# Binary cross entropy over 8192 x 8192: the pieces of the small chunk move from GpSimd's DMA queue to SyncE's

## The chip, the core and the metric

The kernel runs on one core of a Trainium2 chip. A core has a tensor engine (unused here), VectorE (DVE), ScalarE (ACT), GpSimd (POOL) and SyncE (SP), and 16 DMA engines that move data between the chip's memory and the core's on-chip memory (128 partitions). Transfers are issued by an engine into its queue: q0 is the queue that GpSimd feeds by software, q1 the one that SyncE feeds. The metric is the device time of one execution in microseconds (us); the median of three runs is compared.

## The reference

```python
def setup_inputs():
    return {
        "pred": np.random.uniform(0.01, 0.99, (8192, 8192)).astype(np.float32),
        "target": np.random.randint(0, 2, (8192, 8192)).astype(np.float32),
    }

def reference(pred, target):
    eps = 1e-7
    pred = np.clip(pred, eps, 1 - eps)
    return -(target * np.log(pred) + (1 - target) * np.log(1 - pred))
```

Each target is 0 or 1, so each output is -log of the distance |target - 1 + pred|: that is pred where the target is 1 and 1 - pred where it is 0. Two arrays of 268 MB are read and one of 268 MB is written.

## The kernel before

The 8192 x 8192 elements are 524,288 columns on 128 partitions. `plan` (L20 to L27) cuts them into 37 chunks: two halves of 7,680 columns, 32 of 15,360, two halves of 7,680 again and one small one of 2,048. Two rings in on-chip memory hold two big chunks and the small one each: `ring_p` (float32: pred, worked on in place, then the output) and `ring_t` (bfloat16: target, converted by the transfer).

For a chunk, or half of it, `front_of` (L99) does two passes on DVE (L100: clip; L103: t - 1 + p) and two on ACT (L106: absolute value; L107: logarithm), and `back_of` (L109) one on DVE (L110: times -1). `load(k)` issues target and pred of chunk k on GpSimd, but the pred of chunk 0 on SyncE. `store(k)` issues on GpSimd, and on SyncE for the last chunks, k >= n - 3; the two that this concerns are a = 34 and b = 35. The order is written out by hand from L119 on; each engine does its part in this order and waits on semaphores for data, for free places in the rings, and for a semaphore that is used again. There are eight semaphores for the transfers of each of the two queues, taken in turn: the ninth transfer of a queue's turn waits until the first has landed.

In the loop (L133) chunk k is computed in halves and stored whole; behind `store(k)` the load of chunk k + 2 is issued, whose pred part waits for `store(k)` to land, since it takes its place. The small chunk (n - 1) is computed in the loop's turn k = 4.

The small chunk is loaded and stored in another shape. `mixed` (L81) lets partition 8a + b hold row 16b + a of 2,048 columns. Its pred and its output move in uneven pieces ("teeth"): a piece (j, lo, hi) is 32 partitions, 32j to 32j + 31, by columns 256 lo to 256 hi. On the side of the chip's memory it is 4 x 8 rows, on the on-chip side 32. `EARLY` lists the seven pieces of the load (widths in units of 256 columns: 8, 6, 4, 2, then 6, 4, 2), `LATE` the eight of the store (8, 1, 4, 6, 6, 1, 2, 4); either list makes up the small chunk. Before the change the first four loads are issued on GpSimd behind the first three chunks' loads (L122), the last three at L132, behind the load of chunk 3; the eight stores at L152, behind the second half store of z = 33.

The end (L144 to L158): z is computed in halves and stored in halves, a whole, b with its front in halves and its back (L157) and store whole.

Of the kernel before, what the change touches and what calls it, by code (L numbers as in the profile page):

```python
# [1 line left out]

# [4 lines left out]

EPS = 1e-7

BIG = 15 * 1024  # L10
HALF = BIG // 2
STEP = 256
EARLY = ((0, 0, 8), (1, 0, 6), (2, 0, 4), (3, 0, 2), (3, 2, 8), (2, 4, 8), (1, 6, 8))
LATE = (
    (0, 0, 8), (1, 0, 1), (2, 0, 4), (3, 0, 6),
    (1, 2, 8), (1, 1, 2), (3, 6, 8), (2, 4, 8),
)


def plan(total):  # L20

    n, last = divmod(total, BIG)
    assert n > 4 and 0 < last <= 2048
    spots = [(HALF, 0), (HALF, HALF)]
    spots += [(BIG, k % 2 * BIG) for k in range(1, n - 1)]
    end = (n - 1) % 2 * BIG
    return spots + [(HALF, end), (HALF, end + HALF), (last, 2 * BIG)]  # L27

@with_exitstack
def kernel(
    ctx: ExitStack,
    tc: tile.TileContext,
    pred: bass.AP,
    target: bass.AP,
    out: bass.AP,
):
    nc = tc.nc
    fp32 = mybir.dt.float32  # L40
    bf16 = mybir.dt.bfloat16
    Alu = mybir.AluOpType
    Act = mybir.ActivationFunctionType
    P = nc.NUM_PARTITIONS

    R, C = pred.shape
    spots = plan(R * C // P)
    n = len(spots)
    widths = [w for w, _ in spots]
    cols = [sum(widths[:k]) for k in range(n)]  # L50

    def chunk(ap, k):
        flat = ap.rearrange("r c -> (r c)")
        end = R * C - cols[k] * P
        return flat[end - widths[k] * P : end].rearrange("(p w) -> p w", p=P)

    pool = ctx.enter_context(tc.tile_pool(name="rings", bufs=1))
    ring = [P, 2 * BIG + widths[-1]]
    ring_p = pool.tile(ring, fp32, name="ring_p", tag="ring_p")
    ring_t = pool.tile(ring, bf16, name="ring_t", tag="ring_t")  # L60
    warm = pool.tile([1, 8], fp32, name="warm", tag="warm")

    def spot(ring, k, part=(0, 1)):
        w, c = spots[k]
        i, m = part
        return ring[:, c + i * w // m : c + (i + 1) * w // m]

    def load(k):
        queue = nc.sync if k == 0 else nc.gpsimd
        nc.gpsimd.dma_start(out=spot(ring_t, k), in_=chunk(target, k))  # L70
        queue.dma_start(out=spot(ring_p, k), in_=chunk(pred, k))  # L71

    def store(k, part=(0, 1)):
        queue = nc.sync if k >= n - 3 else nc.gpsimd
        i, m = part
        w = widths[k] // m
        queue.dma_start(  # L77
            out=chunk(out, k)[:, i * w : (i + 1) * w], in_=spot(ring_p, k, part)
        )

    def mixed(ap):  # L81
        flat = ap.rearrange("r c -> (r c)")[: widths[-1] * P]
        return flat.rearrange("(b a w) -> a b w", b=8, a=16)

    def tooth_of(ap, j, lo, hi):
        return mixed(ap)[4 * j : 4 * j + 4, :, lo * STEP : hi * STEP]

    def tooth_in(j, lo, hi):
        return spot(ring_p, n - 1)[32 * j : 32 * j + 32, lo * STEP : hi * STEP]

    def load_teeth(teeth):
        for tooth in teeth:
            nc.gpsimd.dma_start(out=tooth_in(*tooth), in_=tooth_of(pred, *tooth))  # L93

    def store_teeth(teeth):
        for tooth in teeth:
            nc.gpsimd.dma_start(out=tooth_of(out, *tooth), in_=tooth_in(*tooth))  # L97

    def front_of(p, t):  # L99
        nc.vector.tensor_scalar(  # L100
            out=p, in0=p, scalar1=EPS, scalar2=1 - EPS, op0=Alu.max, op1=Alu.min
        )
        nc.vector.scalar_tensor_tensor(  # L103
            out=p, in0=t, scalar=1.0, in1=p, op0=Alu.subtract, op1=Alu.add
        )
        nc.scalar.activation(out=p, in_=p, func=Act.Abs)  # L106
        nc.scalar.activation(out=p, in_=p, func=Act.Ln)  # L107

    def back_of(p):  # L109
        nc.vector.tensor_scalar(out=p, in0=p, scalar1=-1.0, scalar2=None, op0=Alu.mult)  # L110

    def front(k, *part):
        front_of(spot(ring_p, k, *part), spot(ring_t, k, *part))

    def back(k, *part):
        back_of(spot(ring_p, k, *part))

    with tc.manual_schedule():
        nc.vector.memset(warm, 1.0)  # L119
        for k in range(3):  # L120
            load(k)
        load_teeth(EARLY[:4])  # L122
        nc.scalar.activation(out=warm, in_=warm, func=Act.Ln)  # L123
        front(0)
        front(1)
        back(0)
        store(0)
        back(1)
        store(1)
        load(3)  # L130
        nc.gpsimd.dma_start(out=spot(ring_t, n - 1), in_=mixed(target))  # L131
        load_teeth(EARLY[4:])  # L132
        for k in range(2, n - 4):  # L133
            front(k, (0, 2))
            front(k, (1, 2))
            back(k, (0, 2))
            back(k, (1, 2))
            store(k)
            for j in range(k + 2, n - 1 if k == n - 5 else k + 3):
                load(j)  # L140
            if k == 4:
                front(n - 1)
                back(n - 1)
        z, a, b = range(n - 4, n - 1)  # L144
        front(z, (0, 2))
        front(z, (1, 2))
        back(z, (0, 2))
        store(z, (0, 2))
        front(a)
        back(z, (1, 2))  # L150
        store(z, (1, 2))
        store_teeth(LATE)  # L152
        front(b, (0, 2))
        front(b, (1, 2))
        back(a)
        store(a)
        back(b)  # L157
        store(b)  # L158


# [1 line left out]
_INS = ['pred', 'target']  # L162
_OUTS = [((8192, 8192), 'float32')]


# [23 lines left out]
```

## Time and profile before

| | |
|---|---|
| median of 3 runs | 1867.51 us (1867.19 to 1867.58) |
| profiled execution | 1866.22 us, span 1864.3 us |
| read and written in the chip's memory | 536.87 MB and 268.44 MB, 432 GB/s over the span |
| one pass over 7,680 columns | L100 4.16, L103 8.16, L110 4.16 us (DVE); L106 6.60, L107 6.60 us (ACT) |
| one pass over 3,840 columns | L100 2.16, L103 4.16 us (DVE); L106 3.39, L107 3.40 us (ACT) |
| big pred load, issue to landing (median) | 35.9 us |
| big store on q0, issue to landing (median) | 29.2 us |
| store of a and of b on q1, issue to landing (median) | 12.8 us |
| pieces: loads, issue to landing | 38.6 to 76.0 us |
| pieces: stores, issue to landing | 10.5 to 16.4 us |

The span is the profiled execution from the first to the last recorded instruction; the time of the execution has 1.9 us more around it. A line of the page's groups has the source line, the engine, the operation, what it writes and reads, the number of instructions, their busy time and mean duration, and the idle time before them with what ended it. In the waits the columns are who waited, for whom, the total in us, how often, and the longest. In a timeline they are start, duration, engine, line, operation and in brackets the idle time before and what ended it; several instructions in a row are merged, so that the duration then reaches from the start of the first to the end of the last. In the table of windows "x" is the number of instructions, and the last two columns are the mean busy share of the 16 DMA engines and what they moved.

### The profile page before, as it was taken

The numbers are of one execution on the slowest core, as the hardware profiler recorded it, in microseconds if no ns is written. First come the engines' busy times: TensorE is split into PE (matmuls) and PEld (weight loads), VectorE is DVE, ScalarE is ACT, GpSimd is POOL, SyncE is SP. The second block draws the span as 40 slices with busy tenths as digits, with TensorE's granted clock in tenths as the row PEclk, the third lists the DMA queues.
The fourth block names the chain that finished last, engine by engine and source line by source line (L and its number), as shares of the span: only waits on it lengthen the run. The fifth ranks groups of instructions, "written<-read, shape, count | busy, mean of one in ns | idle before, by whom it ended". The sixth has DMA issues, their size and how long they took to land.

```text
span 1864.3 us, 640 instructions
## 1 busy us (share of the span) xinstructions
DVE 1122.4 (60%) x210; ACT 900.0 (48%) x142; POOL 68.6 (4%) x126
## 2 busy tenths in 40 slices
DVE  4646676555666555566665556666555766555585
ACT  3345553345554334555433455543345554334555
POOL 1000000000000000000000000000000000000001
DMA  9999999999999999999999999999999999999999
GB/s 295 370 340 353 344 358 380 387 358 351 353 344 358 381 388 362 347 352 345 357 381 388 363 345 355 344 357 383 384 364 345 352 345 357 384 384 365 345 344 390
DMA packets 17620, 671.14 MB, mean 360 GB/s; under 512 B 3152, under 2 KB 3152, under 8 KB 3600
## 3 DMA queue, kind: packets, MB, share of 16 engines
q0 software_dynamic: 17184, 659.31, 98.7%
q1 hardware_dynamic: 432, 11.80, 1.5%
q14 instruction: 4, 0.03, 0.0%
HBM read 536.87 MB, written 268.44 MB: 432 GB/s over the span
## 4 chain that ended last, share of the span: by engine, by line
DMA 35%; issue 25%; ACT 23%; DVE 15%; POOL 1%; POOLq 0%; DVEq 0%; PEldq 0%
DMA ring_p<-in_pred_dram 32%; ACT ring_p L106 12%; ACT ring_p L107 11%; DVE ring_p L103 7%; DVE ring_p L100 4%; DVE ring_p L110 4%; DMA out_dram<-ring_p 3%; POOL ring_t L70 1%; POOL out_dram L77 0%; POOL ring_p L71 0%; POOLq L77 0%; DVEq L100 0%; POOLq L71 0%; PEldq L184 0%; POOLq L70 0%
## 5 line engine op out<-in xcount | busy, mean ns | idle before, releaser
L106 ACT ACTIVATE ring_p<-ring_p 128x7680 f32<-128x7680 f32 (+2 forms) x70 | 450.6, 6437 | 943.1 <-DVE ring_p L103 943.1
L103 DVE SCALAR_TENSOR_TENSOR ring_p<-ring_t,ring_p 128x7680 f32<-128x7680 bf16 (+2 forms) x70 | 557.2, 7960 | 2.4
L100 DVE TENSOR_SCALAR ring_p<-ring_p 128x7680 f32<-128x7680 f32 (+2 forms) x70 | 284.0, 4058 | 395.9 <-DMA ring_p<-in_pred_dram 395.9
L110 DVE TENSOR_SCALAR ring_p<-ring_p 128x7680 f32<-128x7680 f32 (+1 forms) x69 | 284.1, 4117 | 328.9 <-ACT ring_p L107 328.9
L107 ACT ACTIVATE ring_p<-ring_p 128x7680 f32<-128x7680 f32 (+2 forms) x70 | 451.1, 6444 | 2.2
L71 POOL DMA_DIRECT2D ring_p<-in_pred_dram x35 | 18.7, 534 | 921.7 <-DMA out_dram<-ring_p 921.7
L77 POOL DMA_DIRECT2D out_dram<-ring_p x35 | 19.8, 567 | 824.2 <-DVE ring_p L110 799.2
L70 POOL DMA_DIRECT2D ring_t<-in_target_dram x36 | 19.9, 552 | 1.1 <-PEq L184 0.8
L93 POOL DMA_DIRECT2D ring_p<-in_pred_dram x7 | 5.2, 762 | 16.3 <-DMA ring_t<-in_target_dram 16.3
L97 POOL DMA_DIRECT2D out_dram<-ring_p x8 | 4.7, 594 | 12.4 <-DMA out_dram<-ring_p 12.4
L123 ACT ACT_TABLE_LOAD x1 | 1.3, 1283 | 0.7 <-PEq L173 0.7
L131 POOL DMA_DIRECT2D ring_t<-in_target_dram x1 | 0.6, 557 | 0.0
L119 DVE MEMSET warm<- 1x8 f32 x1 | 0.1, 65 | 0.8 <-PEq L173 0.8
L123 ACT ACTIVATE warm<-warm 1x8 f32<-1x8 f32 x1 | 0.2, 207 | 0.0
L173 POOL MEMSET const-float32-0.0<- 128x1 f32 x1 | 0.1, 98 | 0.2 <-issue 0.2
L173 POOL MEMSET const-bfloat16-1.0<- 128x1 bf16 x1 | 0.1, 101 | 0.0
L173 POOL MEMSET const-float32-1.0<- 128x1 f32 x1 | 0.1, 98 | 0.0
L173 POOL MEMSET const-uint8-127<- 128x1 uint8 x1 | 0.1, 98 | 0.0
## 6 DMA issues: line engine op xcount, KB each, us to landing
ring_p<-in_pred_dram POOLq DMA_DIRECT2D x32, 7680.0 KB, 35.9
out_dram<-ring_p POOLq DMA_DIRECT2D x31, 7680.0 KB, 29.2
ring_t<-in_target_dram POOLq DMA_DIRECT2D x32, 3840.0 KB, 46.8
out_dram<-ring_p POOLq DMA_DIRECT2D x4, 3840.0 KB, 29.9
ring_p<-in_pred_dram POOLq DMA_DIRECT2D x3, 3840.0 KB, 35.0
ring_t<-in_target_dram POOLq DMA_DIRECT2D x4, 1920.0 KB, 27.7
out_dram<-ring_p SPq DMA_DIRECT2D x2, 3840.0 KB, 12.8
ring_p<-in_pred_dram SPq DMA_DIRECT2D x1, 3840.0 KB, 18.8
```

The lines of the kernel that those rows point to most:

```text
L70: nc.gpsimd.dma_start(out=spot(ring_t, k), in_=chunk(target, k))
L71: queue.dma_start(out=spot(ring_p, k), in_=chunk(pred, k))
L77: queue.dma_start(out=chunk(out, k)[:, i * w : (i + 1) * w], in_=spot(ring_p, k, part))
L93: nc.gpsimd.dma_start(out=tooth_in(*tooth), in_=tooth_of(pred, *tooth))
L97: nc.gpsimd.dma_start(out=tooth_of(out, *tooth), in_=tooth_in(*tooth))
L100: nc.vector.tensor_scalar(out=p, in0=p, scalar1=EPS, scalar2=1 - EPS, op0=Alu.max, op1=Alu.min)
L103: nc.vector.scalar_tensor_tensor(out=p, in0=t, scalar=1.0, in1=p, op0=Alu.subtract, op1=Alu.add)
L106: nc.scalar.activation(out=p, in_=p, func=Act.Abs)
L107: nc.scalar.activation(out=p, in_=p, func=Act.Ln)
L110: nc.vector.tensor_scalar(out=p, in0=p, scalar1=-1.0, scalar2=None, op0=Alu.mult)
L123: nc.scalar.activation(out=warm, in_=warm, func=Act.Ln)
L131: nc.gpsimd.dma_start(out=spot(ring_t, n - 1), in_=mixed(target))
```

## The change

The pieces are issued by SyncE instead of GpSimd. All seven loads go out at launch, behind SyncE's load of chunk 0; the eight stores go out behind `store(a)` instead of behind the second half store of z. The back and the store of b are done in halves, and the second half of b's front stands behind the back and store of a.

```diff
     def load_teeth(teeth):
         for tooth in teeth:
-            nc.gpsimd.dma_start(out=tooth_in(*tooth), in_=tooth_of(pred, *tooth))
+            nc.sync.dma_start(out=tooth_in(*tooth), in_=tooth_of(pred, *tooth))

     def store_teeth(teeth):
         for tooth in teeth:
-            nc.gpsimd.dma_start(out=tooth_of(out, *tooth), in_=tooth_in(*tooth))
+            nc.sync.dma_start(out=tooth_of(out, *tooth), in_=tooth_in(*tooth))
...
         for k in range(3):
             load(k)
-        load_teeth(EARLY[:4])
+        load_teeth(EARLY)
...
         nc.gpsimd.dma_start(out=spot(ring_t, n - 1), in_=mixed(target))
-        load_teeth(EARLY[4:])
...
         store(z, (1, 2))
-        store_teeth(LATE)
         front(b, (0, 2))
-        front(b, (1, 2))
         back(a)
         store(a)
-        back(b)
-        store(b)
+        store_teeth(LATE)
+        front(b, (1, 2))
+        back(b, (0, 2))
+        store(b, (0, 2))
+        back(b, (1, 2))
+        store(b, (1, 2))
```

In the built program SyncE's queue is then: the load of chunk 0, the seven piece loads, `store(a)`, the eight piece stores, and the two half stores of b. On SyncE's semaphores the eighth piece store waits for `store(a)` to land, the first half store of b for the first piece store, and the second half store for the second piece store. GpSimd's queue has the other loads and stores in the order they had.

## The prediction

> **What bounds the kernel now.** I read the share of the DMA queues first, then the chain of waits, then the windows of the end, then the timeline of SyncE (SP) and GpSimd (POOL) there.
>
> ```profile
> DVE 1122.4 (60%) x210; ACT 900.0 (48%) x142; POOL 68.6 (4%) x126
> q0 software_dynamic: 17184, 659.31, 98.7%
> q1 hardware_dynamic: 432, 11.80, 1.5%
> ```
>
> The 16 DMA engines are busy for the whole span (98.7 + 1.5 is over 100, since the ends of packets overlap a little); no compute engine is above 60%. q0 is POOL's queue, q1 SP's. So a change of the time must come from what the DMA engines carry, or from when they have nothing to carry.
>
> ```profile
> POOL ring_p L71 <- DMA out_dram<-ring_p: 921.7, 32, 35.9
> DVE ring_p L100 <- DMA ring_p<-in_pred_dram: 395.9, 36, 18.7
> SPq L77 <- DMA ring_p<-in_pred_dram: 1715.2, 1, 1715.2
> ```
>
> The compute waits for transfers and the next load waits for the store that frees its place. SP waits 1715 us with nothing to do.
>
> ```profile
> core 0: us, DVE busy (x) ACT busy (x) POOL busy (x), PEclk, DMA share, GB/s
> 1400.00:1454.35 54.35, 32.19 (x7) 26.30 (x4) 1.61 (x3) 1.00 1.00 362
> 1820.00:1837.00 17.00, 15.28 (x5) 16.94 (x4) 5.18 (x8) 1.00 1.01 434
> 1837.00:1845.00 8.00, 4.80 (x2) 7.97 (x3) 0.59 (x1) 1.00 0.91 342
> 1845.00:1860.00 15.00, 4.16 (x1) 1.11 (x1) 0.00 (x0) 1.00 1.01 429
> ```
>
> The first row is one period of the loop (54.35 us for one chunk): full. The end is full too but for 8 us at 0.91. Rows 3 and 5 give an engine's rate: 434 / 16 = 27.1 GB/s.
>
> ```profile
> 1826.33 1.07 POOL L77 DMA_DIRECT2D out_dram<-ring_p  x1 [24.98 <-issue]
> 1827.39 3.53 POOL L97 DMA_DIRECT2D out_dram<-ring_p  x6
> 1834.46 0.60 POOL L97 DMA_DIRECT2D out_dram<-ring_p  x1 [3.54 <-DMA out_dram<-ring_p]
> 1841.83 8.84 SPq L77 DMA_DIRECT2D out_dram<-ring_p  x2
> 1843.89 0.59 POOL L97 DMA_DIRECT2D out_dram<-ring_p  x1 [8.83 <-DMA out_dram<-ring_p]
> ```
>
> The eight store pieces leave from POOL while SP sends the stores of a and b (1841.8 and 1850.3).
>
> **What a piece is worth.** Call 32 rows by 256 columns a unit (32 KiB). The trace's packet records show that a piece of 32 rows runs on four engines, not on 16: the 32 packets of 8,192 bytes of the first load begin in fours (75.18, 75.18, 75.20, 75.29, then 75.48 to 75.60), beside the packets of 6,144 and 4,096 bytes of the next two pieces. So on q0 the pieces that follow each other take different fours. A unit is 8 KiB on each of its four engines: 0.30 us at 27.1 GB/s; the shortest records (309 ns for 8,192 bytes, 234 for 6,144, 159 for 4,096, into which the smaller rows are joined) give 10.0 us for the 32 units of the loads and 10.0 for those of the stores. Going round four groups A to D, the loads give A 8+6, B 6+4, C 4+2, D 2, and the stores, which begin at D, D 8+6, A 1+1, B 4+2, C 6+4: 16 units for each, 5.0 us. The records bear this out: the load of b lands on the 16 engines in four clusters (means 1819.7, 1821.0, 1822.0 and 1824.1), and the last store on all within 2.0 us (1861.45 to 1863.43).
>
> **The change part by part.**
>
> 1. *Issuing.* POOL loses 15 issues of about 0.6 us and a wait of 16.3 us at launch. All of it lay in front of POOL's wait for the first store (issued at 56.8, 32.9 us idle before it) or behind its last big store: 0 us (without that cover 15 x 0.6 = 9 us). SP gains 15 issues of about 0.34 us (its L77 issues: 332 and 342 ns): 2.4 us at launch with SP idle behind it, 2.7 us at the end, see 4.
>
> 2. *Where the loads land.* All seven are on q1 at launch, behind the load of chunk 0, which ends there at 18 us. No row shows a piece on q1; its transfers so far have 128 rows and all 16 engines. The bounds: the pieces are spread as on q0 (0), or every piece starts at the same first engine and so takes the same four (all 64 units there). A turning place must be remembered from one transfer to the next; I take the fixed four as the simplest split of a transfer that knows only its own 32 rows, though the nearest row, q0, turns. Then these four carry 10.0 us of loads where the latest group of before (A) carried 14 units, 4.4 us: every landing that waits for all 16 engines comes 5.6 us later once the pieces are through (about 100 us). The other twelve have nothing of it and run ahead.
>
> Against the row of q0 stands the Trainium skill, DMA: Bandwidth & Descriptors, section "Why a DMA increments its semaphore by 16 and not by 1": a transfer issued through the software path gets consecutive engines from a cursor that goes round, one through the hardware path the lowest-numbered ones, as many as divide the slowest dimensions of both sides, here 4. By the rule the sum is the one below, by q0's row it would be that of the second rival.
>
> 3. *The loop.* Store(k) leaves 43.2 us after chunk k lands (1662.0 to 1705.25), and the period is 54.35: the late engines still have 11.1 us of the next load in their queue then. So the four never run dry. The twelve, up to 10 us ahead, have about 1 us left and may idle, which the time doesn't see. The 5.6 us are carried on, not multiplied.
>
> 4. *The end.* On the four engines the load of b ends at 1825.1 + 5.6 = 1830.7, the two stores of z (9.2 us each) at 1849.1. Compute: a lands at 1812.6, ACT is done with it at 1838.2, DVE with back(a) at 1842.4 (before 1841.8), store(a) leaves and shares the four with the store of z; both done at about 1858.3. DVE then does the second half of b (1842.4 to 1848.7), its first back by 1850.9 and, after ACT at 1855.5, the second by 1857.7. On SP, store(a) is followed by the eight pieces; the eighth waits for the semaphore of store(a), and both halves of store(b) stand behind it and wait besides for the first and second pieces. They leave at about 1861.5 instead of 1851 and 1857.7. That costs the twelve engines, which are idle from 1853, but not the four: these have 10.0 us of pieces until 1868.3 and then 9.2 us of store(b), to 1877.5. So the wait, the halves and the new order of DVE cost 0 as long as the four are late by more than 6.8 us (1868.3 - 1861.5); without that cover, the wait costs 1 to 2 us (second rival).
>
> **The sum.** On the four engines 64 units in place of 16: 20.0 - 5.0 = +15.0 us. The engines of before ended on average at 1862.2 with 0.7 us of idle time in the window at 0.91 (2.75 of 16 engines for 4 us), which the four no longer have: -0.7. Total +14.3; the walk of 4 gives 1877.5 against 1863.1, +14.4. Against the profiled execution (span 1864.3, 1866.2 in all) that is 1880.5; this execution is 1.3 us below the median of 1867.51, so the forecast is 1867.5 + 14.3 = 1881.8. Its bounds: 9.67 us per 32 units at 27.1 GB/s, and 1 us of further idle time at the end won back, give 1880; if q1 doesn't join the rows of 1 and 2 KiB and each costs 159 ns, 24 more packets of each engine are added, 3.8 us: 1885.5. Own range 1878 to 1886.
>
> **The rivals.**
>
> *Loads on one four, stores on another* (a turn that is only made between directions): no engine has over 32 units; +5.0 us, 1872.5. For it: nothing but that the two sides differ in which end has four rows and which has 32.
>
> *The pieces go round or are spread on q1 too*: not slower. For it: q0 does so. Each four again has 16 units, the landings stay, and only the SP wait is left: store(a) can go at 1837 (DVE no longer does the second half of b first), ends on its engines at 1852.7, the eighth piece and both halves follow by 1853.7, start 1.5 us later and end at 1864.4, +1.3 us: 1867 to 1869.5. The point that decides is the fullest engine: 0.31 us a unit above 16, so that with 28 of the 64 units on one four the change would just be seen.
>
> *Faster*: the small packets of q1 slip in beside the large ones and cost nothing, and the idle time goes. That is at most 5.0 + 1.7 us: 1861 to 1864. Against it: from 6 to 18 us q0 and q1 share the engines, and 16.1 packets are under way on the average, no more than with one queue. Without this, 1.7 us of idle time are all there is to win.
>
> **How the numbers follow.** Fixed four 0.80, two fours 0.04, round or spread 0.13, faster 0.03. A measurement tells 0.2% (3.7 us) from no change: faster 0.03, same 0.13, slower 0.84. The fixed four's own range holds about 0.95 of its chance (0.76); with the two fours 0.80, so the range is 1870 to 1886.
>
> **What would show it.** Right: q1 with about 2 MB more; the completions of a load on 16 engines in one group of twelve and one of four, 4 to 10 us later; L71's first loop issues after 98.6 moved by up to 6 us; twelve engines idle at the end and a DMA share well under 1 after 1853; store(b) issued at about 1861; a span near 1878.5. Wrong: landings in one cluster or in four, store(b) issued by 1854, a span below 1867. If the spread at the landings is there but the end is not later, the step of the late stores has failed.

## The result, and the profile after

The changed kernel took 1892.48 us (median of four runs, 1890.72 to 1892.85) against 1867.35 us for the kernel before (1866.83 to 1867.58): a ratio of 1.0133, 95% interval 1.0116 to 1.0151. The forecast was 1881.8 us in a range of 1870 to 1886. The direction and the mechanism named (four engines behind the rest) are there; 10.7 us more were lost, so the time lies outside the range. The span grew by 26.7 us, from 1864.3 to 1891.0, where the sum had 14.3.

The page of the changed kernel, engines and DMA queues:

```profile
DVE 1122.5 (59%) x211; ACT 900.1 (48%) x142; POOL 58.0 (3%) x111
...
q0 software_dynamic: 15408, 657.20, 97.7%
q1 hardware_dynamic: 1116, 13.89, 1.8%
```

2.1 MB went from GpSimd's queue to SyncE's. The computing engines do what they did. The share of the DMA engines is still nearly full over a span that is 27 us longer, though the bytes are the same: part of the new time looks like transfer.

Its waits:

```profile
POOL ring_p L71 <- DMA out_dram<-ring_p: 932.6, 32, 35.0
POOL out_dram L77 <- DVE ring_p L110: 850.5, 35, 58.0
DVE ring_p L100 <- DMA ring_p<-in_pred_dram: 414.0, 36, 18.7
```

DVE waits 18.1 us longer for loads (414.0 against 395.9): the loop is late, by more than the 5.6 us that the sum allowed. SyncE's queue, as a timeline (start, duration):

```profile
0.73 0.40 SPq L71 DMA_DIRECT2D ring_p<-in_pred_dram  x1
1.20 4.87 SPq L93 DMA_DIRECT2D ring_p<-in_pred_dram  x7
1854.77 0.35 SPq L77 DMA_DIRECT2D out_dram<-ring_p  x1
1855.17 15.96 SPq L97 DMA_DIRECT2D out_dram<-ring_p  x8
1873.01 1.36 SPq L77 DMA_DIRECT2D out_dram<-ring_p  x2
```

The halves of store(b) leave at 1873.0, behind the eighth piece, as foreseen. The windows of one turn of the loop and of its end (columns as before: time, busy us and instructions of DVE, ACT and POOL, clock, DMA share, GB/s):

```profile
1400.00:1454.35 54.35, 32.86 (x6) 26.30 (x4) 1.61 (x3) 1.00 1.00 359
...
1843.00:1854.00 11.00, 9.74 (x3) 10.94 (x4) 0.00 (x0) 1.00 0.99 427
1854.00:1865.00 11.00, 9.04 (x4) 7.21 (x3) 0.00 (x0) 1.00 0.92 397
1865.00:1873.00 8.00, 2.16 (x1) 2.88 (x1) 0.00 (x0) 1.00 0.24 101
1873.00:1883.00 10.00, 0.00 (x0) 0.00 (x0) 0.00 (x0) 1.00 0.94 369
1883.00:1891.00 8.00, 0.00 (x0) 0.00 (x0) 0.00 (x0) 1.00 0.25 106
```

From 1865 to 1873 us the share is 0.24, that is four engines of 16: they are at the pieces, and the twelve others have nothing until the halves of store(b) come. From 1883 on the four are alone again.

So the end is as drawn. The rest of the loss is in the loop. GpSimd's timeline of the kernel before there (L71 is the load of pred, issued when the store before it has landed):

```profile
701.50 0.54 POOL L71 DMA_DIRECT2D ring_p<-in_pred_dram  x1 [28.41 <-DMA out_dram<-ring_p]
...
755.84 0.53 POOL L71 DMA_DIRECT2D ring_p<-in_pred_dram  x1 [28.41 <-DMA out_dram<-ring_p]
...
810.18 0.53 POOL L71 DMA_DIRECT2D ring_p<-in_pred_dram  x1 [28.41 <-DMA out_dram<-ring_p]
```

and the same of the changed kernel:

```profile
820.17 0.53 POOL L71 DMA_DIRECT2D ring_p<-in_pred_dram  x1 [28.56 <-DMA out_dram<-ring_p]
845.01 0.54 POOL L77 DMA_DIRECT2D out_dram<-ring_p  x1 [24.32 <-DVE ring_p L110]
...
875.50 0.53 POOL L71 DMA_DIRECT2D ring_p<-in_pred_dram  x1 [29.41 <-DMA out_dram<-ring_p]
900.38 0.54 POOL L77 DMA_DIRECT2D out_dram<-ring_p  x1 [24.35 <-DVE ring_p L110]
...
929.86 0.53 POOL L71 DMA_DIRECT2D ring_p<-in_pred_dram  x1 [28.41 <-DMA out_dram<-ring_p]
```

Before, one turn takes 54.34 us, turn for turn. After, it takes 55.33, then 54.36, and so on: about every second turn is 0.3 to 1.6 us too long. The packet records say where. They don't name the engine, but a packet begins where the last one on its engine ended, so they can be strung on 16 strings. A row of 61,440 bytes takes 2,267 ns (median); each engine moves eight rows of a transfer. In the changed kernel the eighth row often takes 2.4 to 3.5 us (here one of the four late engines and one of the twelve):

```
start us: KiB (ns); s = semaphore
late   298.8:60(2267) 301.1:60(2267) 303.4:60(2267) 305.6:60(3344) 309.0:s(9) 309.0:60(2267)
ahead  255.8:60(2268) 258.0:60(2274) 260.3:60(3312) 263.6:s(7) 263.6:30(2280) 265.9:30(2281)
```

Between 150 and 1790 us this excess over the usual durations is 12.2 us for each engine (before: 0.1 us), 162 of the 194 engine-us of it in eighth rows of pred loads and stores. With the 14.3 us of the sum it makes 26.5 us of the 26.7. The landings show the same on the path: against the kernel before, the last engine of the changed kernel lands its loads 6.2 us later at 254 us and 17.9 us later at the last load but one. So 11.7 us were added inside the loop. The question for the runs was what brings the stretched rows about.

### The profile page after: what moved, and what is told of

Same layout as the page of the kernel before. It is cut to its first block, busy times and chain, and to the rows that moved or that the text cites. A ratio compares the mean times of both kernels' runs of the same rounds, so it can differ in the third digit from the quotient of the medians.

```text
span 1891.0 us, 648 instructions
## 1 busy us (share of the span) xinstructions
DVE 1122.5 (59%) x211; ACT 900.1 (48%) x142; POOL 58.0 (3%) x111
## 4 chain that ended last, share of the span: by engine, by line
DMA 35%; issue 25%; ACT 22%; DVE 15%; POOL 1%; POOLq 0%; DVEq 0%; PEldq 0%
DMA ring_p<-in_pred_dram 32%; ACT ring_p L107 11%; ACT ring_p L106 11%; DVE ring_p L103 8%; DVE ring_p L100 4%; DVE ring_p L110 4%; DMA out_dram<-ring_p 3%; POOL ring_t L70 0%; POOL out_dram L77 0%; POOL ring_p L71 0%; POOLq L77 0%; POOLq L70 0%; DVEq L100 0%; PEldq L185 0%; POOLq L71 0%
## 5 line engine op out<-in xcount | busy, mean ns | idle before, releaser
L100 DVE TENSOR_SCALAR ring_p<-ring_p 128x7680 f32<-128x7680 f32 (+2 forms) x70 | 284.0, 4058 | 414.0 <-DMA ring_p<-in_pred_dram 414.0
L110 DVE TENSOR_SCALAR ring_p<-ring_p 128x7680 f32<-128x7680 f32 (+2 forms) x70 | 284.3, 4061 | 330.4 <-ACT ring_p L107 330.4
L71 POOL DMA_DIRECT2D ring_p<-in_pred_dram x35 | 18.7, 534 | 932.6 <-DMA out_dram<-ring_p 932.6
L77 POOL DMA_DIRECT2D out_dram<-ring_p x35 | 19.2, 549 | 850.5 <-DVE ring_p L110 850.5
## 6 DMA issues: line engine op xcount, KB each, us to landing
out_dram<-ring_p POOLq DMA_DIRECT2D x4, 3840.0 KB, 31.3
```

Of the source, the lines that this page charges most:

```text
L77: queue.dma_start(out=chunk(out, k)[:, i * w : (i + 1) * w], in_=spot(ring_p, k, part))
L100: nc.vector.tensor_scalar(out=p, in0=p, scalar1=EPS, scalar2=1 - EPS, op0=Alu.max, op1=Alu.min)
```

## The experiments

Two theories stood at first. *Skew*: that four engines run some 9 us behind is enough. *Step*: the uneven pieces on GpSimd's queue kept the engines out of step, and without them they reach their eighth rows together. After the first four runs the second became *dry*, later *margin*: what matters is how much work the engines in front still have when the next store is issued. The table has all runs. The margin is the median time from the issue of a store of the loop to the first engine's landing of the load before it; "behind" is the median time from the first to the last engine of that landing; "stretched" is the excess for each engine as above; "b lands" is the load of chunk b. The runs e2, e3 and x1 to x7 are single ones; 19 runs of the kernel before beside e1 to e4 lie within 1.1 us.

| run | margin us | behind us | stretched us | b lands | time us | kernel before, measured beside it |
|---|---|---|---|---|---|---|
| before | 6.0 | 5.1 | 0.1 | 1825.1 | 1867.5 | |
| changed | 2.0 | 9.6 | 12.2 | 1843.2 | 1892.5 | 1867.4 |
| e1_whole | 7.1 | 4.0 | 0.9 | 1824.1 | 1868.4 | 1867.2 |
| e2_loads_back | 5.5 | 5.6 | 0.1 | 1825.1 | 1874.5 | 1867.2 |
| e3_stores_back | 2.1 | 9.4 | 10.7 | 1841.8 | 1887.3 | 1867.2 |
| e4_end_alone | 5.2 | 5.8 | 0.1 | 1825.3 | 1868.1 | 1867.2 |
| x1_after_short | 3.1 | 12.1 | 0.2 | 1832.6 | 1882.4 | 1866.6 |
| x2_before_short | 9.7 | 5.5 | 0.1 | 1825.5 | 1867.0 | 1866.6 |
| x3_before_late | 2.2 | 3.2 | 13.7 | 1842.6 | 1889.7 | 1866.6 |
| x4_eight | 4.6 | 6.5 | 0.1 | 1829.9 | 1872.0 | 1866.6 |
| x5_short_nine | 6.6 | 8.7 | 0.1 | 1831.7 | 1881.5 | 1867.0 |
| x6_eight_late | 2.2 | 3.4 | 14.9 | 1846.1 | 1889.7 | 1867.0 |
| x7_half | 4.5 | 6.6 | 0.3 | 1829.8 | 1879.6 | 1867.0 |
| x8_halves | 12.2 (first half) | 12.0 | 1.2 | 1833.6 | 1883.1 | 1867.1 |

**The parts of the change, one at a time.** e1_whole takes the four engines away: one transfer of 128 rows each way.

```diff
-        for tooth in teeth:
-            nc.sync.dma_start(out=tooth_in(*tooth), in_=tooth_of(pred, *tooth))
+        nc.sync.dma_start(out=spot(ring_p, n - 1), in_=mixed(pred))
...
-        for tooth in teeth:
-            nc.sync.dma_start(out=tooth_of(out, *tooth), in_=tooth_in(*tooth))
+        nc.sync.dma_start(out=mixed(out), in_=spot(ring_p, n - 1))
```

> The changed kernel, but the small chunk moves in one transfer of 128 rows each way on SyncE (all 16 DMA engines), at the same two places. It computes the same output. Nothing puts four engines behind. Theory skew (the loop gets slower because four engines run some 9 us behind the other twelve): every loop period is 54.35 us again, the load of b lands at about 1823 to 1825 us, the span is 1862 to 1866 us. Theory step (the loop gets slower because engines reach the end of their eight rows at the same moment, which the uneven pieces on GpSimd's queue prevented): all 16 are in step, so the eighth packets of loads and stores stretch as in the changed kernel, the loop loses 10 to 13 us and the span is 1873 to 1879 us.

1868.39 us, ratio 1.0007 (0.9998 to 1.0017). Step alone costs little: all engines land the small chunk within 1 us of each other (30.5 to 31.3 us), some eighth rows stretch (0.9 us for each engine), the engines drift to 4 us apart, and from about 730 us on next to nothing stretches. The span, 1866.2 us, is 0.2 us over the range of skew. So step is no lasting state of its own accord; skew was still open.

e2_loads_back puts the seven loads back on GpSimd; the stores and the end are the changed kernel's.

```diff
-            nc.sync.dma_start(out=tooth_in(*tooth), in_=tooth_of(pred, *tooth))
+            nc.gpsimd.dma_start(out=tooth_in(*tooth), in_=tooth_of(pred, *tooth))
...
-        load_teeth(EARLY)
+        load_teeth(EARLY[:4])
...
+        load_teeth(EARLY[4:])
```

> The changed kernel with the seven piece loads back on GpSimd at their two places; the stores of the pieces and the end as in the changed kernel. Both theories: the loop is that of the kernel before (periods 54.35 us, load of b landing at about 1825 us). The end alone is then priced: the eight piece stores on one fixed four (10.0 us of them) behind store(a), span 1867 to 1875 us, depending on which of the four clusters of the loads this four is. If the span stays under 1866 us, the pieces of the stores don't all take the same four.

1874.52 us, +7.4: the price of the stores on one four, behind `store(a)` as in the changed kernel. The last engine of the twelve ends at 1866.1, the four at 1869.8 to 1871.1. The loop is clean.

e3_stores_back moves the loads alone (the kernel before with L93 on SyncE and `load_teeth(EARLY)` at L122).

> Only the seven piece loads move to SyncE at launch; the piece stores stay on GpSimd and the end is that of the kernel before. Theories skew and step both: the loop is that of the changed kernel (every second period or so 0.3 to 1.6 us too long, load of b landing 15 to 20 us late, at 1840 to 1845 us). The piece stores go round the four groups, so the fixed four get 2 to 14 of their units instead of 32: span 1877 to 1886 us, below the 1891 us of the changed kernel by the part of the end. If the loop has its 54.35 us again, the place of the loads is not what slows it.

1887.32 us; span (1885.5) and landing of b (1841.8) lie in the ranges. The loop loses 10.7 us for each engine: the place of the loads is what slows it.

e4_end_alone has the new order of the end and the halves alone.

```diff
         front(b, (0, 2))
-        front(b, (1, 2))
         back(a)
         store(a)
-        back(b)
-        store(b)
+        front(b, (1, 2))
+        back(b, (0, 2))
+        store(b, (0, 2))
+        back(b, (1, 2))
+        store(b, (1, 2))
```

> The kernel before with the new order of the end alone: back and store of a in front of the second half of b, the last store in halves; all pieces on GpSimd as before. Every theory: the loop is unchanged; store(a) leaves at 1837 instead of 1841.8 us, the halves of store(b) at about 1845 and 1852 us. Of the 0.7 us of idle time in the window of 1837 to 1845 us and the 1.0 us at the end a part is won: span 1862.5 to 1865 us, time 1866 to 1868 us, no difference that counts.

1868.06 us, ratio 1.0005 (0.9996 to 1.0015): nothing that counts, by itself. The span, 1866.1 us, is 1.1 us over the expected range: none of the idle time was won.

**Skew or margin.** x1_after_short leaves out the multiplication by -1 for the second half of each chunk of the loop (these outputs keep the other sign), so that each store of the loop leaves 4.2 us earlier. The engines get no closer, but those in front keep more work.

```diff
             back(k, (0, 2))
-            back(k, (1, 2))
             store(k)
```

> The changed kernel, but the multiplication by -1 is left out for the second half of each chunk of the loop (32 passes of 4.16 us; these outputs keep the other sign), so that each store leaves 4.2 us earlier. Theory dry (the twelve engines that run ahead empty their queue before the next store is issued, start again at one moment and so stay in step; the stretched eighth packets follow from that): with 15.3 us in place of 11.1 us left in the queue of the four late engines the twelve keep 5 to 6 us, don't run dry, drift apart, and the loop loses at most 4 us in place of 12.2: landing of the load of b at 1828 to 1835 us, span 1876 to 1883 us. Theory skew (four engines 9 us behind are enough): nothing changes, landing at 1841 to 1845 us, span 1888 to 1892 us.

```profile
782.55 0.54 POOL L77 DMA_DIRECT2D out_dram<-ring_p  x1 [20.14 <-ACT ring_p L107]
...
816.22 0.53 POOL L71 DMA_DIRECT2D ring_p<-in_pred_dram  x1 [32.60 <-DMA out_dram<-ring_p]
836.89 0.54 POOL L77 DMA_DIRECT2D out_dram<-ring_p  x1 [20.14 <-ACT ring_p L107]
...
870.57 0.53 POOL L71 DMA_DIRECT2D ring_p<-in_pred_dram  x1 [32.60 <-DMA out_dram<-ring_p]
```

GpSimd's timeline of this run: the turn is 54.35 us again (816.22 to 870.57). The four are further behind than in the changed kernel (12.1 us) and nothing stretches: 10 us are won, and the time of 1882.37 us is nearly the forecast. Skew falls. The margin that decided was 3.1 us, less than the 5 to 6 of the expectation.

x2_before_short leaves out the same in the kernel before.

> The kernel before with the same multiplication left out in the loop: the control. Both theories: the transfers bound the loop already, so nothing is won by a shorter computation; periods 54.35 us, span 1863 to 1865 us.

1866.99 us against 1866.59, span 1865.1 (0.1 over the range): a shorter computation wins nothing there.

x3_before_late is the other way round: the kernel before, with stores that leave 6.3 us later.

```diff
             back(k, (1, 2))
+            for part in ((1, 2), (3, 4)):
+                p = spot(ring_p, k, part)
+                nc.vector.tensor_scalar(out=p, in0=p, scalar1=1.0, scalar2=None, op0=Alu.mult)
             store(k)
```

> The kernel before with two more passes of DVE (times 1.0, over 7,680 and 3,840 columns, 6.3 us) in front of each store of the loop; same output. Each store leaves 6.3 us later: the latest engines still have 4.8 us in their queue, but the first ones, 4.4 to 5 us ahead, have about 0 and run dry. Theory dry: the first engines restart in step, their eighth packets stretch, and the loop loses 4 to 12 us: span 1868 to 1877 us. Theory skew: the engines are no further apart than before, periods 54.35 us, span 1863 to 1866 us. If the latest engines run dry too, the periods grow by a constant amount in every turn, which would be seen apart from stretched packets.

```profile
762.21 0.54 POOL L71 DMA_DIRECT2D ring_p<-in_pred_dram  x1 [22.83 <-DMA out_dram<-ring_p]
793.44 0.54 POOL L77 DMA_DIRECT2D out_dram<-ring_p  x1 [30.70 <-DVE ring_p L140]
...
816.77 0.54 POOL L71 DMA_DIRECT2D ring_p<-in_pred_dram  x1 [22.25 <-DMA out_dram<-ring_p]
848.00 0.54 POOL L77 DMA_DIRECT2D out_dram<-ring_p  x1 [30.70 <-DVE ring_p L140]
...
871.76 0.53 POOL L71 DMA_DIRECT2D ring_p<-in_pred_dram  x1 [22.69 <-DMA out_dram<-ring_p]
```

Uneven turns (54.56, 54.99) in the kernel before, with 13.7 us of stretched rows and a span of 1887.7 us, 11 us above what was expected at most: no piece had been moved, and no engine was further behind than before. Of the 23.4 us more in the span 17.5 lie ahead of the landing of b (1842.6 for 1825.1 us): mostly the stretched rows, and some 2.3 us of empty engines between 216 and 324 us, where the computation of the small chunk makes one store later still. The other 5.9 us lie behind that landing and were not followed up.

x4_eight puts eight engines behind instead of four (e1_whole with its load in two pieces of 64 rows, whose side in the chip's memory has 8 x 8 rows).

```diff
-        nc.sync.dma_start(out=spot(ring_p, n - 1), in_=mixed(pred))
+        for j in range(2):
+            nc.sync.dma_start(
+                out=spot(ring_p, n - 1)[64 * j : 64 * j + 64, :],
+                in_=mixed(pred)[8 * j : 8 * j + 8],
+            )
```

> The kernel of the first experiment of this study (whole transfers of the small chunk on SyncE), but its load in two pieces of 64 rows. By the split seen so far each piece takes eight engines, the same eight: these have 5.0 us of it, the other eight none. Neither group runs dry (6 us are left to the eight in front). Theory dry: as in the run with 128 rows, a few us of stretched packets until the engines have drifted apart, landing of the load of b at 1823 to 1828 us, span 1864 to 1870 us. Theory skew: a loss in proportion, about half of the 12.2 us, landing at 1829 to 1834 us, span 1870 to 1876 us.

Nothing stretches (0.1 us); the span of 1869.9 us is at the edge of the one range and the landing, 1829.9, at the start of the other. That expectation had left out that eight engines with 16 units land later than the 8 units of e1_whole by themselves; this gives 2.5 of the 5.8 us between the two landings, and what gives the rest is open. It isn't the loop: against the kernel before the loads land 3.5 us later at 251 us and 3.4 us later at the last load but one, and the turns are 54.35 us. No skew loss.

x5_short_nine is x1_after_short with about 28% of the columns loaded in one transfer of 128 rows, to bring the four back to the 9 us of the changed kernel.

```diff
+        w = 576
+        nc.sync.dma_start(out=spot(ring_p, n - 1)[:, :w], in_=mixed(pred)[:, :, :w])
+        for j in range(4):
+            nc.sync.dma_start(
+                out=spot(ring_p, n - 1)[32 * j : 32 * j + 32, w:],
+                in_=mixed(pred)[4 * j : 4 * j + 4, :, w:],
+            )
```

> The run of the changed kernel with the multiplication of the second half left out in the loop, but the first 576 of the small chunk's 2,048 columns are loaded in one transfer of 128 rows and the other 1,472 in four pieces of 32 rows, so that the four engines are about 2.8 us less behind: some 9 us, as they were in the changed kernel, with 15.3 us in their queue when the store is issued. Theory dry: the twelve keep 6 us, nothing runs dry, periods 54.35 us, the load of b lands at about 1829 us, span 1876 to 1879 us. Theory skew, in the form that just the 9 us are harmful (the run before had 12 us): eighth packets stretch as in the changed kernel, landing at 1838 to 1843 us, span 1885 to 1891 us.

8.7 us behind, 0.1 us stretched: it isn't that just this distance is harmful. The span, 1879.7, is 0.7 us above the range, and b lands at 1831.7 for 1829; this is not from the loop, since the loads are 5.7 us late at 253 us and 5.7 us late at the last load but one.

x6_eight_late is x4_eight with the later stores of x3_before_late.

> The run with the load of the small chunk in two pieces of 64 rows (eight engines 6.5 us behind, loop undisturbed), with the two more passes of 6.3 us in front of each store of the loop; same output. The eight late engines keep 4.8 us in their queue, the eight in front have nothing and run dry by 2 to 4 us. Theory dry: stretched eighth packets as in the changed kernel, the loop loses 8 to 20 us, span 1878 to 1892 us. Theory skew: nothing new against 1869.9 us, span 1869 to 1872 us.

14.9 us stretched, 1889.7 us: +17.7 against x4_eight for a computation that is 6.3 us longer and was hidden there.

x7_half is the changed kernel with w = 1024 in the edit of x5_short_nine.

> The changed kernel with half of the small chunk's columns loaded in one transfer of 128 rows and half in four pieces of 32 rows, the rest as it is; same output. The four engines are some 6 to 7 us behind instead of 9 to 11, so the twelve have 4 us when the store is issued. Theory dry: the loop keeps 54.35 us, and the sum of the prediction holds: 52 units on the fixed four in place of 16, +11.1 us less 0.7, span 1873 to 1876 us. Theory skew: two thirds of the 12.2 us are lost besides, span 1881 to 1885 us.

The loop is clean (0.3 us stretched, margin 4.5 us). The span, 1877.9 us, lies between both ranges, 1.9 us above the first; the load of b lands 2.8 us later than its 20 units give (1825.1 + 6 x 0.31 = 1827.0), and what makes that was not found; stretched rows it isn't, since the loads are 2.8 us late at 251 us already and 3.2 us at the last load but one.

x8_halves leaves the computation as it is and gives the margin in another way. The rows of its stores are half as long.

```diff
             back(k, (0, 2))
+            store(k, (0, 2))
             back(k, (1, 2))
-            store(k)
+            store(k, (1, 2))
```

> The changed kernel with each store of the loop in halves, the first half issued as soon as its half of the chunk is ready, some 13 us before the second; same output. In the changed kernel the store is issued 2.0 us (median) before the first engine has landed the load in front of it; here the engines in front have 9 us of store in their queue when the second half comes. Theory margin (the loop loses time where this margin is under about 2.5 us): periods 54.35 us and the time of the runs with an earlier store, span 1878 to 1882 us, time 1880 to 1884 us. Theory skew (four engines 9 us behind are enough): the loss of 12.2 us stays, span 1888 to 1893 us. If the halves bring a price of their own (twice the store issues and completions in the loop), the periods show it as a constant.

```profile
787.56 0.54 POOL L77 DMA_DIRECT2D out_dram<-ring_p  x1 [12.59 <-DVE ring_p L110]
...
817.35 0.54 POOL L71 DMA_DIRECT2D ring_p<-in_pred_dram  x1 [28.72 <-DMA out_dram<-ring_p]
828.75 0.54 POOL L77 DMA_DIRECT2D out_dram<-ring_p  x1 [10.86 <-DVE ring_p L110]
841.88 0.54 POOL L77 DMA_DIRECT2D out_dram<-ring_p  x1 [12.59 <-DVE ring_p L110]
...
871.74 0.53 POOL L71 DMA_DIRECT2D ring_p<-in_pred_dram  x1 [28.79 <-DMA out_dram<-ring_p]
```

1883.05 us (1882.96 to 1883.15), ratio to before 1.0086 (1.0069 to 1.0103), 9.4 us below the changed kernel with the same pieces on the same queue. The turn is 54.39 us, 1.2 us are stretched, and the four are 12 us behind. No run beat the kernel before.

## Why the prediction was wrong

*What bounds the kernel*: right. *Where the pieces land*: right; the fixed four was the fullest in every run with pieces of 32 rows on q1. The completions of the first load piece on SyncE show one update 1.2 us after the issue and four more at 30.5 to 30.7 us, and the loads behind it land in a group of twelve and one of four (pred of chunk 1: twelve at 40.35 to 41.05, four at 45.17 to 45.36). So the rule of the Trainium skill, DMA: Bandwidth & Descriptors, section "Why a DMA increments its semaphore by 16 and not by 1", that the hardware path takes the lowest-numbered engines, agrees with the trace in that all pieces took the same four; the records don't name engines, so which four they are it doesn't show. q0's row was the wrong one to go by. The rivals of two fours and of a round were out; the 64 units cost about what they were said to: the 5.6 us of the loads measured 6.2 us at 254 us, the stores alone cost 7.4 us (e2_loads_back), and all together cost 16.0 us where the loop was nearly clean (x8_halves), for the 14.3 of the sum. The upper bound's 3.8 us for rows that aren't joined were mis-sized without effect: the rows were not joined, but a packet of 1,024 bytes took 46 ns and one of 2,048 bytes 84 ns instead of 159.

*Issuing*: a size was off without effect. A piece costs SyncE 0.70 us at launch (seven in 4.87 us) instead of 0.34. At the end the first seven leave over some 9 us, in front of a store that had to wait longer anyway.

*The loop*, step 3, failed. It said of the twelve engines that they "have about 1 us left and may idle, which the time doesn't see", and that the 5.6 us "are carried on, not multiplied". The four were never empty, as said. But with 2.0 us between the issue of a store and the end of the queue in front, the eighth rows of all 16 engines stretched, those of the four too, and that put about 12 us on the path. Nine runs stand behind this: wherever the margin was 3.1 us or more nothing of weight stretched (x1, x4, x5, x7, and x8 with its first halves), whether the engines were 6.5 or 12 us apart; where it was 2.0 to 2.2 us they lost 10.7 to 14.9 us (the changed kernel, e3, x3, x6), also with engines only 3 us apart and without any moved piece (x3). The margin is the turn less the time from a landing to its store (43.3 us here, 39.1 in x1, 49.7 in x3) less the distance between the engines. So it can be set by the computation, by the distance or by an earlier store, and each of the three ended the loss. The 2.0 to 2.2 us are the medians at which the slow loops settled, with single turns of the later loop from 0.9 to 2.4 us; x3 began at 5.2 us and came down to -0.3 us within three turns. They are not a threshold that was set and measured. The prediction had the 11.1 us of the late engines and the 1 us of the early ones side by side and gave a price only to the first.

*The end*: right. From the landing of b to the last engine it took 46.3 us (1843.2 to 1889.5), drawn as 46.8 (1830.7 to 1877.5); the halves left 29.8 us after the landing, drawn as 30.8. The wait of the eighth piece for store(a) cost the twelve 8 us and the time nothing. The halves and the order alone: no difference (e4_end_alone).

What isn't settled is why it is the eighth row that stretches and why on the engines that do have work. e1_whole shows the same at a margin of 7 us while the engines are in step, and it ends there as they drift apart; at a small margin the engines in front all start the next store when it arrives (in x3 and x6 the 16 engines were pulled together to about 3 us). It would be easy to say that step stretches the rows and that the small margin keeps the step. But in x5 and x7 the twelve engines in front landed within about 0.6 us of each other all along the loop and next to nothing stretched (0.1 and 0.3 us), while in the later turns of the changed kernel they were some 3 us apart and rows did. So step among the engines in front isn't enough, and the cause inside the engines stays open.

## What to carry to other kernels

When a change makes some DMA engines late, ask of the others how much they still have when the next transfer is issued: here loops with 3.1 us or more lost next to nothing, and loops that settled at 2.0 to 2.2 us lost 11 to 15 us; in the changed kernel the four late engines, which end the waits, always had work. Pieces of few rows go to few engines, and on SyncE's queue to the same ones; their sum over the fullest engine is the price, not their bytes over 16. A pattern that spreads load by where the queue stands next belongs to that queue.

## What the runs showed of the hardware

- A queue that is kept full by the profile's share can still lose time: stretched rows count as busy. The share over a turn (1400 to 1454.35 us) is 1.00 in the clean loop and in the slow one, with 362 and 359 GB/s.
- From the issue of a store on GpSimd to its first packet on an empty engine it took 1.2 us (1010.26 to 1011.43 and 1339.11 to 1340.28 us in the changed kernel), and 1.1 us in x3 (1452.39 to 1453.50). It took 1.6 us at 242.83 us, where the issue itself lasted longer (0.96 us); that is the only place where the twelve engines of the changed kernel were seen empty for long (17.7 engine-us of 25.2 in all).
- On SyncE's queue rows of 1,024 and 2,048 bytes stay packets of their own, 46 and 84 ns; on GpSimd's queue they were joined to packets of 4,096 bytes, 159 ns at the shortest, which is a little less by the byte.
- Two pieces of 64 rows whose side in the chip's memory is 8 x 8 rows take eight engines, both the same eight (x4_eight: 6.5 us behind).
